# Where adding loads and other loads stand in the queues, and diagonal blocks masked by selects instead of products

## The chip, the cores and the metric

The kernel runs on one core of one Trainium2 chip. A core has five engines that run side by side, each through its own queue in order: TensorE (matrix products; PE in the rows below, its weight loads PEld), VectorE (DVE), ScalarE (ACT), GpSimd (POOL) and SyncE (SP). SyncE and GpSimd issue the transfers, which 16 DMA engines carry out. The metric is the device time of one execution in microseconds (us); lower is better. The kernel before takes 1485.59 us, the median of three runs (1484.99 to 1488.79).

## What is computed

A trunk of two layers on 512 positions of width 1024. Layer 0 mixes with an mLSTM, layer 1 with stick-breaking attention; each layer then cross-attends into 256 memory rows and applies a SwiGLU FFN. Each of these parts is normalised before and behind. Cut to the mixer that the change touches and to the frame:

```python
def reference(x, mem, ...):
    mem_n = rms_norm(mem, mem_norm_gain)
    for layer in range(2):
        hn = rms_norm(x, g[0])
        y = mlstm_mixer(hn, ...) if layer % 2 == 0 else stick_breaking_mixer(hn, ...)
        x = x + rms_norm(y, g[1])
        x = x + rms_norm(memory_cross_attention(rms_norm(x, g[2]), mem_n, ...), g[3])
        x = x + rms_norm(swiglu_ffn(rms_norm(x, g[4]), ...), g[5])

def mlstm_mixer(h, w_in, b_gate, head_gain, w_out):     # 4 heads, q and k 128 wide, v 256 wide
    q, k, v, o, gates = split(h @ w_in)                 # gates: 4 input, 4 forget, capped at 15
    ...                                                 # in each head, with b the running sum of log forget:
    # d[t, s] = exp(b_t - b_s + i_s - m_t) for s <= t, and 0 above the diagonal
    # num = ((q k^T) * d) v,  den = sum_s of (q k^T) * d,  out = num / max(|den|, exp(-m_t))
    return (rms_norm(out) * sigmoid(o)) @ w_out
```

The zero above the diagonal of `d` is the mask that the change makes in another way.

## The kernel before

Products are in fp32r, each factor split into a high part and a residual (`split`: a cast on ScalarE, a subtraction of 128x1024 on VectorE, "residual" below), so that a product is three matmuls.

**Units of seven products.** Large projections are cut into blocks of two by two and done with seven block products in place of eight, by `seven()`; there are 37 such units, numbered as they begin (mLSTM 0 to 4, cross-attention of layer 0 5 and 6, FFN of layer 0 7 to 20, then layer 1). A unit needs sums of weight blocks. It loads w00, w10 and w11 (128x1024 each, SyncE's queue) and forms the sums in place:

```python
self.gather(t1, src(1, 0))          # t1 = w00: DMA that adds w01 onto it, on GpSimd's queue
self.tt(t2, t1, w11, ALU.add)       # t2 = t1 + w11, VectorE
...
self.gather(t3, src(1, 0))          # t3 = w11: second adding DMA
...
if number in BY_DMA:
    self.gather(w10, t2)            # w10 += t2, by an adding DMA
else:
    self.tt(w10, w10, t2, ALU.add)  # or on VectorE
```

These DMAs are called adding loads here. The second one overwrites w11, so it can only be issued when t2 and the two halves of the old w11 have been formed. What it lands is split, and TensorE multiplies it.

**What sets the order.** The program isn't written in the order of its queues. `Plan` records every operation with its engine, a duration and the buffers that it reads and writes. `deadlines()` gives each a due time, counted back from the TensorE product that needs it; a load gets 2.5 us on top. `lay_out()` then fills each engine's queue by due time, as soon as inputs and a free buffer are there. The durations are the planner's own; on the chip an instruction waits only for what it reads, for its buffer and for its place in the queue.

**The mLSTM.** `MORDER` is the order in which its parts are written out; each letter advances one part by a step: `q`, `r` the projections of q and k for two heads each (units 0 and 2), `V` and `v` the values (unit 1 and a plain projection), `s` the scores of one head, `h` the heads' outputs for a block of 128 positions, `o` and `P` the two halves of the output gate (units 3 and 4). A unit has three steps. Then follow the loads and products of w_out.

**Masks and scores.** `masks()` makes constant tiles with `memset`, a select on GpSimd (it keeps or fills elements by their index) and a cast. One of them, `above`, holds a large number above the diagonal. `scores(hh)` needs for each pair of 128-blocks exp(-(row value) + column value). A product with `pick` spreads the row values of the head over the partitions, for blocks off the diagonal into one bank (384 columns), for those on it into a second (512 columns), onto which a product of the identity with `above` (512 columns) adds the large number, so that the exponential gives 0:

```python
self.mms([(mb[:, P:], self.pick[:, hh], rows[:, P:], True, True)])
self.mms([(md, self.pick[:, hh], rows, True, False), (md, self.ident_r, self.above, False, True)])
```

ScalarE takes ten exponentials of 128x128 per head from these banks; VectorE multiplies them with the products of q and k. There are eight banks (`ps`) in all.

Lines of the profile: L526 and L540 are TensorE's products and transposes, L470 VectorE's sums and products of two tiles, L482 its operations with a scalar in between, L448 and L455 ScalarE's functions and casts, L437 an adding load's issue, L432 another load's, L508 a select.

## Time and profile before

| | |
|---|---|
| median of three runs | 1485.59 us (1484.99 to 1488.79) |
| profiled execution, its device time | 1486.58 us |
| span of the profile | 1484.9 us |
| TensorE busy | 1469.4 us |
| VectorE busy | 1197.8 us |
| ScalarE busy | 865.8 us |
| GpSimd busy | 143.6 us |
| mean granted clock of TensorE | 0.997 of full speed |

The profile is one execution. Its span runs from the first instruction to the last; the device time lies 1.7 us above it. Busy time counts an engine's work, not its waits nor the issuing of DMAs from SyncE. The granted clock is given as a share: 1.00 is 2.4 GHz, 0.50 is 1.2 GHz. "Idle before" is the time that an engine stood still ahead of an instruction, with what ended it.

### The profile page before, as it was taken

What the parts mean: (1) busy time and instruction counts of PE and PEld (TensorE: products, weight loads), DVE (VectorE), ACT (ScalarE), POOL (GpSimd) and SP (SyncE); (2) the same over time, 40 slices, a digit from 0 to 9 for tenths busy, and PEclk for the clock granted to TensorE, in tenths of its full rate; (3) what the DMA queues carried; (4) which work ended last, traced back from release to release, by engine and by line L of the source; (5) the groups of instructions that cost most, each with busy time, mean ns of one, the idle gap of its engine ahead of it and who ended that gap; (6) DMA issues with size and microseconds to landing.
All of it is one profiled execution on the core that took longest, in us unless ns stands there. A gap on an engine that the chain in (4) does not pass through costs nothing.

```text
span 1484.9 us, 26101 instructions
## 1 busy us (share of the span) xinstructions
PE 1469.4 (99%) x10335; PEld 1370.6 (92%) x10335; DVE 1197.8 (81%) x1851; ACT 865.8 (58%) x1495; POOL 143.6 (10%) x179
## 2 busy tenths in 40 slices
PE   9999899999999999999999999999999999999998
PEld 7999889998999999998889889888988999999996
DVE  7988879887787877897838998878787968778985
ACT  7768656564654554544538997766546644444632
POOL 3100100100011111110100001001000111110100
PEclk9999999999999999999999999999999999999999
DMA  8445646532655575675343459255414563854741
GB/s 224 90 100 143 199 135 206 108 121 85 174 110 128 96 161 129 137 189 162 110 113 93 99 164 254 102 174 126 140 63 132 119 142 72 213 114 100 152 161 57
DMA packets 173228, 200.43 MB, mean 135 GB/s; under 512 B 8241, under 2 KB 142129, under 8 KB 173106
## 3 DMA queue, kind: packets, MB, share of 16 engines
q1 hardware_dynamic: 126192, 131.65, 28.8%
q0 software_dynamic: 46912, 67.12, 23.3%
q8 instruction: 81, 1.33, 0.4%
q14 instruction: 41, 0.34, 0.1%
q10 hardware_dynamic: 2, 0.00, 0.0%
HBM read 176.20 MB, written 10.49 MB: 126 GB/s over the span
## 4 chain that ended last, share of the span: by engine, by line
PE 94%; DMA 2%; DVE 2%; ACT 1%; issue 1%; DVEq 0%; POOL 0%; POOLq 0%; ACTq 0%
PE ps L526 92%; PE ps L540 2%; DMA big<-in_ffn_w_down_dram 1%; DVE big L470 1%; DMA big<-in_ml_w_in_dram 1%; ACT big L455 0%; DVE big L482 0%; ACT half L448 0%; DMA big<-in_norm_gains_dram 0%; DVE sm L475 0%; DVE half L470 0%; DVE sm L482 0%; ACT sm L448 0%; DVE big L456 0%; ACT half L455 0%
## 5 line engine op out<-in xcount | busy, mean ns | idle before, releaser
L526 PE MATMUL ps<-big,big 128*128 128x256 f32 (+2 forms) x9762 | 1407.4, 305 | 5.8 <-ACT big L455 2.8
L526 PEld LDWEIGHTS ps<-big,big 128*128 128x128 f32 (+1 forms) x9762 | 1298.0, 188 | 91.1 <-ACT big L455 3.3
L470 DVE TENSOR_TENSOR big<-big,big 128x1024 fp32r<-128x1024 f32 (+2 forms) x541 | 626.4, 1191 | 45.7 <-ACT big L455 25.1
L455 ACT CAST big<-big 128x1024 fp32r<-128x1024 f32 (+1 forms) x422 | 417.6, 1021 | 162.2 <-DMA big<-in_ffn_w_gate_up_dram 45.2
L470 DVE TENSOR_TENSOR big<-ps,big 128x512 fp32r<-128x512 f32 (+3 forms) x197 | 114.4, 605 | 44.2 <-ACT big L455 31.5
L455 ACT COPY half<-ps 128x512 f32<-128x512 f32 (+1 forms) x112 | 65.5, 585 | 124.1 <-PE ps L526 116.4
L455 ACT CAST big<-ps 128x512 fp32r<-128x512 f32 (+1 forms) x159 | 76.9, 513 | 99.6 <-PE ps L526 64.8
L448 ACT ACTIVATE half<-ps 128x512 f32<-128x512 f32 (+2 forms) x137 | 79.4, 581 | 90.2 <-PE ps L526 84.6
L448 ACT ACTIVATE half<-big 128x512 bf16<-128x512 f32 (+2 forms) x64 | 42.1, 659 | 73.0 <-DVE big L470 45.9
L437 POOL DMA_DIRECT2D big<-in_ffn_w_gate_up_dram x40 | 51.1, 1278 | 316.9 <-DVE big L470 217.4
L470 DVE TENSOR_TENSOR big<-half,big 128x512 fp32r<-128x512 f32 (+4 forms) x126 | 76.6, 625 | 5.9 <-ACT big L448 3.3
L482 DVE SCALAR_TENSOR_TENSOR half<-ps,half 128x512 f32<-128x512 f32 (+3 forms) x74 | 47.0, 645 | 36.4 <-PE ps L526 18.0
L455 ACT CAST big<-half 128x512 fp32r<-128x512 f32 (+3 forms) x82 | 43.9, 558 | 10.7 <-DVE half L470 6.3
L470 DVE TENSOR_TENSOR half<-ps,half 128x512 f32<-128x512 f32 (+1 forms) x54 | 36.4, 687 | 15.4 <-PE ps L526 11.9
L448 ACT ACTIVATE big<-ps 128x512 fp32r<-128x512 f32 (+2 forms) x66 | 39.6, 612 | 15.2 <-PE ps L526 11.8
L470 DVE TENSOR_TENSOR big<-ps,gain 128x512 f32<-128x512 f32 x32 | 22.0, 687 | 31.8 <-ACT half L448 30.0
L540 PE MATMUL ps<-const,big 128*128 128x128 f32 (+1 forms) x314 | 41.9, 270 | 0.8 <-DVE big L482 0.8
L540 PEld LDWEIGHTS ps<-const,big 128*128 128x128 f32 (+1 forms) x314 | 36.0, 140 | 6.0 <-DVE big L482 1.1
L475 DVE TENSOR_SCALAR sm<-sm,sm 128x1 f32<-128x1 f32 x101 | 24.2, 243 | 20.2 <-ACT half L448 11.4
L448 ACT ACTIVATE half<-half 128x512 f32<-128x512 f32 (+1 forms) x50 | 30.8, 630 | 10.3 <-DVE half L470 10.2
L482 DVE SCALAR_TENSOR_TENSOR big<-big,sm,gain 128x512 f32<-128x512 f32 (+1 forms) x45 | 34.9, 808 | 0.6
L482 DVE SCALAR_TENSOR_TENSOR big<-big,sm,big 128x512 f32<-128x512 f32 (+1 forms) x49 | 34.1, 737 | 0.8
(92 smaller groups left out, 588.2 us busy)
## 6 DMA issues: line engine op xcount, KB each, us to landing
big<-in_ffn_w_gate_up_dram SPq DMA_DIRECT2D x68, 512.0 KB, 5.0
big<-in_ffn_w_gate_up_dram POOLq DMA_DIRECT2D x40, 512.0 KB, 6.1
big<-in_ffn_w_down_dram SPq DMA_DIRECT2D x36, 512.0 KB, 5.9
big<-in_xa_w_kv_dram SPq DMA_DIRECT2D x32, 512.0 KB, 5.4
big<-in_sb_w_qkv_dram SPq DMA_DIRECT2D x24, 512.0 KB, 4.1
big<-big SPq DMA_DIRECT2D x80, 128.0 KB, 2.3
big<-in_ml_w_in_dram SPq DMA_DIRECT2D x18, 512.0 KB, 5.3
dr<-big POOLq DMA_DIRECT2D x16, 512.0 KB, 4.2
```

The costliest lines, as they stand in the source:

```text
L437: "POOL", 1040, lambda nc: nc.gpsimd.dma_start(ap(out), ap(in_), accum_op=ALU.add), [in_, out], [out], load=ns
L448: nc.scalar.activation(ap(out), ap(in_), func, scale=ap(scale), **kw)
L455: "ACT", 0.833 * n + (60 if psum else 95), lambda nc: nc.scalar.copy(ap(out), ap(in_)), [in_], [out],
L470: self._dve(out, [a, b], lambda nc: getattr(nc, q).tensor_tensor(out=ap(out), in0=ap(a), in1=ap(b), op=op), eng)
L475: nc.vector.tensor_scalar(out=ap(out), in0=ap(a), scalar1=ap(s1), scalar2=ap(s2), op0=op0, **kw)
L482: lambda nc: nc.vector.scalar_tensor_tensor(out=ap(out), in0=ap(a), scalar=ap(s), in1=ap(b), op0=op0, op1=op1),
L526: nc.tensor.matmul(ap(out), lhsT=ap(a), rhs=ap(b), start=start, stop=stop, **kw)
L540: nc.tensor.transpose(ap(out), ap(in_), ap(ident))
```

## The change

Three things are edited.

The planner's treatment of loads: an adding load's due time moves forward by `ahead` (6.5 us in the mLSTM, 4 in cross-attention, 7 in layer 0's FFN, 0.5 in layer 1's). Behind an adding load, a load of another kind that is due more than `NEAR` (11.75 us) ahead is laid out no sooner than 2 us before the adding load's planned end. Both are rules of the planner: the program gets no wait for them, only another order of its queues and other buffers.

Tables: in `MORDER` the second step of `o` stands ahead of the last head's scores, not behind it. `BY_DMA` gains units 0, 27 and 31. `LEAD` of the cross-attention's output loads goes from 3000 to 2000 (the entry 'cross', also edited, isn't read).

The mask: `above` is gone with its select and cast. `scores()` makes one product with `pick` over 512 columns into one bank, takes all exponentials from it, and a select on GpSimd sets each diagonal block's part above the diagonal to 0: four per head, 16 in all, 128x128 each. TensorE's instructions go from 10335 to 10327.

```diff
-MORDER = '+qqVqrsVVrrssosoohhPhhPP'
+MORDER = '+qqVqrsVVrrssoosohhPhhPP'
-BY_DMA = (3, 4, 18, 38, 39)
+BY_DMA = (0, 3, 4, 18, 27, 31, 38, 39)
+NEAR = 11750
+AHEAD = {'mlstm': 6500, 'cross': 4000, 0: 7000, 1: 500}
-LEAD = {'stick': 14000, 'ffn': 0, 'cross': 0, 'ml_out': 5500, 'sb_out': 2000, 'xa_out': 3000}
+LEAD = {'stick': 14000, 'ffn': 0, 'cross': 2000, 'ml_out': 5500, 'sb_out': 2000, 'xa_out': 2000}
...
     def deadlines(self):
-                o.rank = min(s.rank - (0 if s.eng == "PE" else s.ns) - 150 for s in o.succ) - o.ns - (2500 if o.load else 0)
+                o.rank = min(s.rank - (0 if s.eng == "PE" else s.ns) - 150 for s in o.succ) - o.ns - (2500 + o.ahead if o.load else 0)
...
     def lay_out(self):
             t = max(free[e], o.ready)
+            if o.load and e in ("SP", "POOL") and not o.adds and o.rank > headrank + NEAR:
+                t = max(t, quiet)
...
                 o.end = wire + 1500
+                if o.adds:
+                    quiet = o.end - 2000
...
     def gather(self, out, in_, ns=2800):
             "POOL", 1040, lambda nc: nc.gpsimd.dma_start(ap(out), ap(in_), accum_op=ALU.add), [in_, out], [out], load=ns
         )
+        self.plan.ops[-1].adds, self.plan.ops[-1].ahead = True, self.ahead
...
     def masks(self, behind):
-        self.above = self.half(NT, P, dt=R)
         self.strict = self.const(P, 2, P, dt=R)
-        for m, op, fill in ((self.above, ALU.is_ge, BIG), (self.strict, ALU.is_gt, -BIG)):
-            raw = self.half(*m.idx.shape)
-            self.memset(raw, 0.0, behind=[behind])
-            self.select(raw, op, fill, 0, [[0, m.idx.shape[0]], [1, P]], -1)
-            self.copy(m, raw)
+        raw = self.half(2, P)
+        self.memset(raw, 0.0, behind=[behind])
+        self.select(raw, ALU.is_gt, -BIG, 0, [[0, 2], [1, P]], -1)
+        self.copy(self.strict, raw)
...
         def scores(hh):
-            mb, md = self.bank(), self.bank()
-            self.mms([(mb[:, P:], self.pick[:, hh], rows[:, P:], True, True)])
-            self.mms([(md, self.pick[:, hh], rows, True, False), (md, self.ident_r, self.above, False, True)])
+            mb = self.bank()
+            self.mms([(mb, self.pick[:, hh], rows, True, True)])
...
                 for i in range(j, NT):
-                    src = (md if i == j else mb)[:, i * P : (i + 1) * P]
-                    self.act(dec[:, (i - j) * P : (i - j + 1) * P], src, AF.Exp, scale=-1.0, bias=col[(i, j)][:, hh : hh + 1])
+                    to, src = dec[:, (i - j) * P : (i - j + 1) * P], mb[:, i * P : (i + 1) * P]
+                    self.act(to, src, AF.Exp, scale=-1.0, bias=col[(i, j)][:, hh : hh + 1])
+                    if i == j:
+                        self.select(to, ALU.is_ge, 0.0, 0, [[1, P]], -1)
```

**GpSimd's queue in the mLSTM, units o and P.** In the kernel before, `big_1328` and `big_1281` are w11 and w10 of unit o, `big_1552`, `big_1666` and `big_1680` are w00, w10 and w11 of unit P, and `big_1950` is its t2.

```order
L437 DMA big_1328<-in_ml_w_in_dram 128x4x256
L437 DMA big_1281<-big_1455 128x1024
L437 DMA big_1552<-in_ml_w_in_dram 128x4x256
L437 DMA big_1666<-big_1950 128x1024
L437 DMA big_1680<-in_ml_w_in_dram 128x4x256
L432 DMA big_2060<-in_mem_dram 128x1024
L432 DMA big_2099<-in_mem_dram 128x1024
L432 DMA big_2116<-in_x_dram 128x1024
```

In the changed kernel w11 and w10 of unit o are `big_1305` and `big_1318`; of unit P w00, w10, w11 and t2 are `big_1607`, `big_1660`, `big_1676` and `big_1937`.

```order
L445 DMA big_1305<-in_ml_w_in_dram 128x4x256
L445 DMA big_1318<-big_1458 128x1024
L517 AFFINE_SELECT half_1582<-half_1582 128x128
L517 AFFINE_SELECT half_1613<-half_1613 128x128
L445 DMA big_1607<-in_ml_w_in_dram 128x4x256
L445 DMA big_1676<-in_ml_w_in_dram 128x4x256
L445 DMA big_1660<-big_1937 128x1024
L440 DMA big_2050<-in_mem_dram 128x1024
L440 DMA big_2095<-in_mem_dram 128x1024
```

Unit P's load onto w11 has moved ahead of its sum into w10, and selects now stand among the adding loads.

**VectorE's queue around unit P's t2.** In the kernel before, the rows onto `big_1617` are the last products of a heads' block, those onto `sm_1895` the denominators of the next block; `big_1950` is t2, and `big_1985` the residual of w11.

```order
L482 SCALAR_TENSOR_TENSOR big_1617<-ps_1800,sm_1857,gain_581 128x256
L470 TENSOR_TENSOR half_1878<-ps_1880,half_1878 128x512
L482 SCALAR_TENSOR_TENSOR sm_1895<-ps_1920,const_821 128x1
L470 TENSOR_TENSOR sm_1895<-ps_1920,sm_1895 128x1
L470 TENSOR_TENSOR big_1950<-big_1552,big_1680 128x1024
L482 SCALAR_TENSOR_TENSOR sm_1895<-ps_1937,const_821 128x1
L470 TENSOR_TENSOR sm_1895<-ps_1937,sm_1895 128x1
L482 SCALAR_TENSOR_TENSOR sm_1895<-ps_1956,const_821 128x1
L470 TENSOR_TENSOR sm_1895<-ps_1956,sm_1895 128x1
L492 RECIPROCAL sm_1980<-sm_1895 128x4
L470 TENSOR_TENSOR big_1985<-big_1680,big_1925 128x1024
```

In the changed kernel these are `big_1632`, `sm_1963`, `big_1937` (t2) and `big_1904` (the residual).

```order
L479 TENSOR_TENSOR big_1904<-big_1676,big_1876 128x1024
L491 SCALAR_TENSOR_TENSOR big_1632<-ps_1781,sm_1859,gain_574 128x256
L491 SCALAR_TENSOR_TENSOR big_1632<-ps_1793,sm_1859,gain_574 128x256
L479 TENSOR_TENSOR big_1937<-big_1607,big_1676 128x1024
L479 TENSOR_TENSOR half_1879<-ps_1863,half_1879 128x512
L491 SCALAR_TENSOR_TENSOR sm_1963<-ps_1900,const_814 128x1
L491 SCALAR_TENSOR_TENSOR sm_1963<-ps_1918,const_814 128x1
L491 SCALAR_TENSOR_TENSOR sm_1963<-ps_1933,const_814 128x1
L479 TENSOR_TENSOR sm_1963<-ps_1900,sm_1963 128x1
L491 SCALAR_TENSOR_TENSOR sm_1963<-ps_1947,const_814 128x1
```

The residual of w11 now stands ahead of t2, and both ahead of the next block's denominators.

**GpSimd's queue at the end of layer 0's FFN.** In the kernel before, rows from `in_ffn_w_down_dram` are the last units' adding loads, those from `dr` loads of the residual of x.

```order
L437 DMA big_7486<-in_ffn_w_down_dram 128x4x256
L437 DMA big_7492<-in_ffn_w_down_dram 128x4x256
L437 DMA big_7524<-in_ffn_w_down_dram 128x4x256
L432 DMA big_7845<-dr_4290 128x1024
L432 DMA big_7878<-dr_4409 128x1024
L432 DMA big_7911<-dr_4520 128x1024
L437 DMA big_7508<-in_ffn_w_down_dram 128x4x256
L432 DMA big_7939<-dr_4691 128x1024
```

In the changed kernel:

```order
L445 DMA big_7487<-in_ffn_w_down_dram 128x4x256
L445 DMA big_7493<-in_ffn_w_down_dram 128x4x256
L445 DMA big_7525<-in_ffn_w_down_dram 128x4x256
L445 DMA big_7509<-in_ffn_w_down_dram 128x4x256
L440 DMA big_7891<-dr_4288 128x1024
L440 DMA big_7930<-dr_4407 128x1024
L440 DMA big_7969<-dr_4518 128x1024
L440 DMA big_8002<-dr_4685 128x1024
```

The last adding load of w_down (`big_7508`, now `big_7509`) has moved ahead of three loads of the residual of x.

## Rows read from the trace of the kernel before

**Rows 1.** Page, part 1: busy us (share of span) and instructions of each engine.
```profile
PE 1469.4 (99%) x10335; PEld 1370.6 (92%) x10335; DVE 1197.8 (81%) x1851; ACT 865.8 (58%) x1495; POOL 143.6 (10%) x179
```

**Rows 2.** Stretches: us, busy us (count) per engine, PEclk, DMA share, GB/s.
```profile
120.00:140.00 20.00, 19.88 (x167) 19.67 (x166) 16.93 (x56) 17.02 (x37) 1.27 (x1) 1.00 0.62 150
160.00:180.00 20.00, 15.40 (x98) 14.22 (x97) 14.52 (x31) 15.79 (x28) 0.53 (x1) 0.83 0.62 232
680.00:700.00 20.00, 19.12 (x117) 16.94 (x118) 17.35 (x22) 9.61 (x13) 0.00 (x0) 1.00 0.40 134
1460.00:1480.00 20.00, 17.86 (x95) 15.11 (x93) 12.07 (x33) 5.41 (x18) 0.00 (x0) 1.00 0.14 53
```

**Rows 3.** Timeline of TensorE: start, us, what, [idle before <-releaser].
```profile
164.43 0.58 PE L526 MATMUL ps<-big,big 128*128 128x256 f32 x1 [2.81 <-ACT big L455]
165.69 5.23 PE L526 MATMUL ps<-big,big 128*128 128x256 f32 x23 [0.68 <-DVE big L470]
171.59 5.99 PE L526 MATMUL ps<-big,big 128*128 128x256 f32 x48 [0.67 <-ACT half L455]
```

**Rows 4.** Stretches of 6 and 8 us at unit P.
```profile
158.00:164.00 6.00, 3.17 (x27) 2.73 (x25) 3.44 (x10) 1.10 (x3) 0.53 (x1) 0.99 1.10 343
164.00:172.00 8.00, 6.22 (x27) 5.68 (x28) 5.73 (x7) 7.71 (x15) 0.00 (x0) 0.58 0.86 349
```

**Rows 5.** Chain of waits up to 166 us: start, us, what.
```profile
150.17 13.14 DMA big<-in_ml_w_in_dram
...
163.33 1.05 ACT big L455
...
164.41 1.24 DVE big L470
```

**Rows 6.** Timeline of VectorE, same columns as rows 3.
```profile
143.24 0.87 DVE L482 SCALAR_TENSOR_TENSOR big<-ps,sm,gain 128x256 f32<-128x256 f32 x2
...
146.48 1.23 DVE L470 TENSOR_TENSOR big<-big,big 128x1024 f32<-128x1024 f32 x1
```

**Rows 7.** Timeline of GpSimd's issues, same columns.
```profile
114.12 1.26 POOL L437 DMA_DIRECT2D big<-in_ml_w_in_dram  x1 [8.81 <-DVE half L482]
...
148.36 0.87 POOL L437 DMA_DIRECT2D big<-big  x1 [13.89 <-ACT half L448]
```

**Rows 8.** DMA issues, 148 to 171: count, KB each, median us to landing.
```profile
big<-in_x_dram POOLq DMA_DIRECT2D x4, 512.0 KB, 13.2
big<-in_mem_dram POOLq DMA_DIRECT2D x2, 512.0 KB, 13.7
...
big<-in_ml_w_in_dram POOLq DMA_DIRECT2D x1, 512.0 KB, 13.1
```

**Rows 9.** DMA issues, 112 to 126 (unit o).
```profile
big<-in_ml_w_in_dram POOLq DMA_DIRECT2D x1, 512.0 KB, 5.9
big<-big POOLq DMA_DIRECT2D x1, 512.0 KB, 8.1
```

**Rows 10.** DMA issues, 666 to 682 (end of FFN of layer 0).
```profile
big<-in_ffn_w_down_dram POOLq DMA_DIRECT2D x1, 512.0 KB, 10.9
big<-dr POOLq DMA_DIRECT2D x1, 512.0 KB, 11.9
```

**Rows 11.** Chain of waits: a projection of 48 products, 512 wide.
```profile
358.66 11.13 PE ps L526 x48
```

**Rows 12.** Chain of waits ahead of unit P's first product.
```profile
137.14 0.40 DVE big L482
...
137.59 8.09 PE ps L526 x66
```

**Rows 13.** Groups of GpSimd: line, engine, what xcount | busy us, mean ns | idle.
```profile
L508 POOL TENSOR_SCALAR_AFFINE_SELECT half<-half 128x128 f32<-128x128 f32 x2 | 0.6, 286 | 0.0
```

**Rows 14.** Stretch in which the masks are made.
```profile
22.00:28.00 6.00, 6.00 (x40) 5.36 (x39) 6.00 (x8) 3.78 (x8) 5.86 (x10) 1.00 0.73 121
```

**Rows 15.** Timeline of ScalarE: the last head's exponentials.
```profile
116.56 2.89 ACT L448 ACTIVATE half<-ps,const 128x128 f32<-128x128 f32 x10 [0.45 <-PE ps L526]
```

More of the change, by code (lines that the diff above doesn't have):

```diff
@@ L140 @@
 class Op:
-    __slots__ = ("eng", "ns", "fn", "deps", "succ", "rank", "bufs", "news", "table", "wait", "start", "end", "load", "seq", "ready", "base", "alts", "lead")
+    __slots__ = ("eng", "ns", "fn", "deps", "succ", "rank", "bufs", "news", "table", "wait", "start", "end", "load", "seq", "ready", "base", "alts", "lead", "ahead", "adds")
 class Plan:
@@ L167, in op @@
         o.rank = o.base = self.pe + self.bias
-        o.lead = self.lead
+        o.lead, o.adds, o.ahead = self.lead, False, 0
         o.deps, o.succ, o.bufs, o.news = set(), [], [], []
@@ L213, in lay_out @@
         free = dict.fromkeys(self.LATENCY, 0.0)
-        table, wire = "ln_exp", 0.0
+        table, wire, quiet = "ln_exp", 0.0, 0.0
         cand = {e: [] for e in free}
@@ L395, in __init__ @@
         self.kept = None
-        self.sevens = 0
+        self.sevens = self.ahead = 0
     def big(self, *shape, dt=F32):
@@ L1686, in after_mixer @@
             nxt["f"](n, t, ps)
+        k.ahead = AHEAD["mlstm"]
         if layer % 2 == 0:
@@ L1700, in after_cross @@
             nxt2["f"](n, t, ps)
+        k.ahead = AHEAD["cross"]
         k.cross(XORDER[layer], h, nxt["m"], kt, filler, xa_w_q[layer], xa_w_kv[layer], xa_w_o[layer], after_cross)
@@ L1714, in after_ffn @@
             return k.boundary(xs, g(layer, 5), g(layer + 1, 0), nxt3["h"], ys=ys, spill=nxt3["x"])
+        k.ahead = AHEAD[layer]
         k.ffn(UNITS[layer], h, ffn_w_gate_up[layer], ffn_w_down[layer], after_ffn, layer == depth - 1)
```

## Prediction

> **What bounds the kernel now.** I read the busy times first: TensorE 1469.4 of 1484.9 us, VectorE 1197.8 [rows 1]. TensorE sets the time, so the question for every edit is whether it takes work from TensorE or closes one of its gaps. The gaps add up to 1484.9 - 1469.4 = 15.5 us. The stretches of 20 us say where they are [rows 2]: 4.6 us between 160 and 180, 0.9 between 680 and 700, 0.1 between 120 and 140, 2.1 between 1460 and 1480, and the last 4.9 us, in which TensorE is done. The change doesn't touch the tail, so two places count.
>
> The first is mLSTM unit P, the output gate's second half. TensorE stops at 161.6, starts one matmul at 164.43, goes on at 165.69 and once more at 171.59 [rows 3]. Its clock is 0.99 up to 164 and 0.58 on average in the eight us behind [rows 4], so for much of them it ran at 1.2 GHz; just before, it had stood still. There 23 matmuls took 5.23 us, 227 ns each; 48 of the same kind from 171.59 on took 5.99 us, 125 ns each [rows 3]. The low clock cost 23 x (227 - 125) = 2.4 us, and the place 4.6 + 2.4 = 7.0 us.
>
> The chain of waits says who is late: the second adding load of unit P (the DMA that adds w01 onto w11) is issued at 150.17 and takes 13.14 us; then come a cast of 1.05 and a subtraction of 1.24 [rows 5]. Why 150.17? VectorE must form the sum t2 from w11 before the load overwrites it, and did so at 146.48 [rows 6], behind rows of the heads; then came the residual of w11, and on GpSimd's queue the sum into w10 at 148.36 [rows 7]. Why 13.14? Two loads of mem and four of x were under way in those 23 us beside others, and those of x were as slow (13.2 us) [rows 8]. The same kind of load in unit o, issued at 114.12 [rows 7], landed in 5.9 us [rows 9].
>
> The second place is the end of layer 0's FFN: the 0.9 us of idle time lie behind an adding load of w_down that took 10.9 us, with a load of the residual beside it [rows 10].
>
> **The change part by part.**
>
> *Unit P.* The orders show it: the residual of w11 and t2 now stand ahead of block 2's denominators on VectorE, and the load onto w11 ahead of the sum into w10 on GpSimd. In the trace the four head products that stay ahead of t2 ended at 144.1 [rows 6]. With the residual in front (1.2 us, the length of a 1024-wide row [rows 6]) t2 would run from about 145.3 to 146.5 and the load be issued at about 147, 3 us sooner. Its landing I bound by 5.9 us (unit o) and 13.14 us (as now) [rows 5, 9]: 153 to 160. With 1.05 + 1.24 us and hand-overs the data are there between 155.5 and 162.7. TensorE arrives at 161.6, or at some 161 with the work below gone. So the stop of 4.6 us becomes 0 to 1.8 us. I take 0.3, near unit o's row: there too the sum into w10 was the neighbour, and the loads of mem and x stay behind both on GpSimd's queue. The stop of 0.9 us at 680 left the clock at 1.00 [rows 2], so I take the 2.4 us as regained. Gain: 7.0 - 0.3 = 6.7 us, bounds 5.2 and 7.0.
>
> That loads are "held back" is a rule of the planner; no wait for it is put into the program. It acts only through the order of each queue and the buffers that the plan picks, so I give it no gain of its own.
>
> *FFN of layer 0.* The last adding load of w_down stood behind three loads of the residual and now stands ahead of all four. Gain 0 to 0.9 us; I take 0.8.
>
> *Masks.* Per head the products of 384 and 512 columns with `pick` and of 512 columns with the identity become one of 512. Four of 512 and four of 384 go. At the pace of a 512-wide projection, 48 in 11.13 us or 232 ns [rows 11], that is 4 x 0.232 + 4 x 0.174 = 1.6 us of TensorE's work. It is of use only if nothing else sets the pace behind. At 137.59 the first product of unit P started right behind a VectorE row of the heads that frees a bank [rows 12], and TensorE had 0.1 us of idle time there [rows 2]: that row was only just late. TensorE now arrives 1.6 us sooner, the rows of VectorE and ScalarE that lead to it hardly do. I let 1.0 of the 1.6 us be given back there (bounds 0 and 1.6). Net gain: 0.6 us.
>
> *Selects.* Sixteen selects of 128x128 come to GpSimd, each between ScalarE's exponential and VectorE's product. One takes 0.29 us [rows 13], 4.6 us in all on an engine that is a tenth busy [rows 1]. The heads read the scores some ten us or more behind, and each head holds a bank less than now. I cost them at nothing; that distance is the cover. Without it each is 0.29 us and a hand-over of some 0.1: 16 x 0.4 = 6.4 us at most. The adding loads that queue behind them are the rival below.
> One of the two selects of that size ran beside the mask work between 22 and 28, where VectorE was busy 6.00 of 6 us [rows 14]; the mean of both is 0.29 us all the same. The Trainium skill, "SBUF — State Buffer", section "SBUF: two separate sides", speaks against this edit: GpSimd and VectorE share a pair of ports that one instruction locks for its whole length, a VectorE instruction with two SBUF inputs among them, and the other engine waits. By it each select could wait for a 1024-wide row, some 20 us on GpSimd in all, or hold VectorE up for 4.6 us; the rows of this size show no such wait, and off TensorE's path the sum would be the same.
>
> *Three more sums by DMA.* Units 0, 27 and 31 leave their sum into w10 to a DMA; VectorE saves 1.23 us each [rows 6], where it isn't the bound. The cost is an issue on GpSimd and a DMA beside the unit's second adding load, which in unit o landed in 5.9 us with such a neighbour [rows 9]. I take nothing, and up to 1 us of loss each at 27 and 31, where the sum is queued ahead of that load. All other loads that move: nothing, and up to 2 us of loss together, for the range.
>
> **Sum.** Against the profiled execution: 1484.9 - 6.7 - 0.8 - 0.6 = 1476.8 us of span. That execution took 1.7 us more than its span and 1.0 us more than the median of the three runs. Against the median: 1485.6 - 8.1 = 1477.5 us.
>
> **The rivals.**
> *The load stays slow.* The same bytes go through the same DMA engines, which had hardly a free moment from 158 on [rows 4]. If the load still takes 13 us and t2 comes no sooner, only its place in the queues (1 to 2 us) is won; the stop is then some 3 us and the clock falls again: 1485.6 - 2 - 0.8 - 0.6 = 1482. For it: the landing times of x [rows 8]; against it: those loads now queue behind. Chance 0.14.
> *The gap moves.* VectorE was busy 14.5 us between 160 and 180 [rows 2]; with 7 us less, that work must fit into 13 us, or TensorE stops for the splits of w_out instead, with the low clock behind. If the place gives back 6 us: 1483.5. Against it: part of that work belongs to the projection behind and can be done there. Chance 0.08.
> *Slower.* The adding loads of units r, o and P now queue behind selects, and a select waits for its exponential. In unit o the load was issued at 114.12 [rows 7], while the last head's ten exponentials ran only from 116.56 to 119.45 [rows 15]. A load held until then is up to 5.3 us late; if TensorE waits as long and then runs at the low clock (2.4 us), that is 7.7 us. At one load it eats the gain (1485); at two the kernel is slower: 1477.5 + 15.4 = 1493. It decides from 12.5 us of such losses. Against it: in the new order the last head's product with `pick` stands right behind the third's, so its exponentials can run sooner. Chance 0.05.
> *The change doesn't do what it says:* waits that no plan sees swallow the moves, and only the masks' 0.6 us stay, 1485. Chance 0.05.
>
> **How the numbers follow.** The forecast has 0.68: 1477.5, its own range 1474.8 (less if nothing is given back at the bank) to 1480.5 (a stop of 1.8 us and a loss at other loads). 0.3% is 4.5 us, about what a measurement of this kernel can tell from no change, so faster means under 1481.1 and slower over 1490.1. Faster: 0.68 and half of the slow load's 0.14, 0.75. Slower: 0.05. Same: 0.20. The range leaves out the slower case, half of the last one and some 0.05 below: 1474.5 to 1485.
>
> **What would show it.** Right: between 155 and 175 TensorE idles under 1 us and its clock stays at 1.00; the adding load of unit P is issued some 3 us sooner against TensorE's work and lands in under 10 us; no idle time near 680; about 1 us of idle time ahead of unit P's first product; 16 selects of about 0.3 us. Wrong: a clock under 1.00 anywhere but the start and the tail, or an adding load of unit o or P issued right behind a select that waited.

## The result

The changed kernel takes 1477.84 us, the median of six runs (1476.74 to 1482.79); the kernel before took 1485.36 in its six (1484.98 to 1488.79). The ratio is 0.9950, with a 95% interval of 0.9934 to 0.9966: 7.4 us less (5.1 to 9.8). The forecast was 1477.5, within 1474.5 to 1485.0.

The profile after, first its part 1 (columns as in rows 1), its span being 1476.3 us:

```profile
PE 1465.3 (99%) x10327; PEld 1367.7 (93%) x10327; DVE 1197.2 (81%) x1854; ACT 864.5 (59%) x1490; POOL 155.6 (11%) x196
```

TensorE's busy time fell by 4.1 us, its idle time from 15.5 to 11.0. Three stretches of 20 us, beside rows 2:

```profile
120.00:140.00 20.00, 18.98 (x159) 18.76 (x158) 17.58 (x53) 18.84 (x41) 3.37 (x3) 1.00 0.57 126
160.00:180.00 20.00, 20.00 (x141) 18.43 (x140) 19.72 (x53) 15.30 (x31) 0.53 (x1) 1.00 0.70 263
680.00:700.00 20.00, 20.00 (x103) 16.77 (x102) 14.95 (x31) 8.21 (x22) 0.54 (x1) 1.00 0.15 52
```

Between 160 and 180 TensorE no longer stops and its clock stays at 1.00, where 4.6 us of idle time and 0.83 stood. Between 120 and 140 it now stands still for 1.0 us. The timeline of TensorE shows both, beside rows 3:

```profile
138.45 24.53 PE L535 MATMUL ps<-big,big 128*128 128x256 f32 x204 [1.02 <-DVE big L491]
162.82 1.47 PE L549 MATMUL ps<-const,big 128*128 128x128 f32 x12
164.05 5.91 PE L535 MATMUL ps<-big,big 128*128 128x256 f32 x48
169.80 1.47 PE L549 MATMUL ps<-const,big 128*128 128x128 f32 x12
171.03 3.73 PE L535 MATMUL ps<-big,big 128*128 128x512 f32 x15
```

138.45 is unit P's first product, 171.03 the first of w_out; in the kernel before these stood at 137.59 [rows 12] and 178.21. GpSimd's issues there, beside rows 7, and unit P's second adding load among the DMA issues from 145 to 171, beside rows 8:

```profile
147.53 1.28 POOL L445 DMA_DIRECT2D big<-in_ml_w_in_dram  x1 [12.99 <-DVE big L479]
148.28 1.43 POOL L445 DMA_DIRECT2D big<-big  x1
151.53 0.98 POOL L440 DMA_DIRECT2D big<-in_mem_dram  x1 [1.81 <-PE ps L535]
```

```profile
big<-in_ml_w_in_dram POOLq DMA_DIRECT2D x1, 512.0 KB, 6.1
```

The load is issued ahead of the sum into w10, 9.1 us behind unit P's first product in place of 12.6 [rows 5, 12], and lands in 6.1 us in place of 13.14.

**Where the time is counted.** The first 37 to 40 us of the program, in which its first loads arrive, differ by up to 3 us from profile to profile whatever the kernel, and what comes behind the mLSTM (from the first product of w_out to the last product) lay between 1298.3 and 1300.2 us in all fourteen profiles, with a kernel made from the one before at either end (e5 and e1). I therefore also compare one stretch: from the product behind the short wait that every profile shows near 38 (37.09 in the kernel before, 38.60 in the changed one) to the first product of w_out. It took 178.21 - 37.09 = 141.1 us before and 171.03 - 38.60 = 132.4 after: 8.7 us less. Profiles of three kernels with the same order of queues there (the changed one, e6 and e12) gave 132.43, 132.47 and 132.43, so it tells tenths apart.

### The profile page after: what moved, and what is told of

The parts are those of the page before. It is cut to its first block, busy times and chain, and to the rows that moved or that the text cites. A ratio compares the mean times of both kernels' runs of the same rounds, so it can differ in the third digit from the quotient of the medians.

```text
span 1476.3 us, 26092 instructions
## 1 busy us (share of the span) xinstructions
PE 1465.3 (99%) x10327; PEld 1367.7 (93%) x10327; DVE 1197.2 (81%) x1854; ACT 864.5 (59%) x1490; POOL 155.6 (11%) x196
## 3 DMA queue, kind: packets, MB, share of 16 engines
q8 instruction: 81, 1.33, 0.4%
## 4 chain that ended last, share of the span: by engine, by line
PE 97%; DVE 1%; ACT 1%; issue 0%; DVEq 0%; POOL 0%; ACTq 0%; POOLq 0%
PE ps L535 95%; PE ps L549 2%; DVE big L479 0%; DVE big L491 0%; ACT big L464 0%; ACT half L457 0%; DVE sm L484 0%; ACT L358 0%; ACT sm L457 0%; DVE sm L491 0%; DVE big L465 0%; DVEq L1753 0%; ACTq L440 0%; ACT const L464 0%; POOL half L512 0%
## 5 line engine op out<-in xcount | busy, mean ns | idle before, releaser
L479 DVE TENSOR_TENSOR big<-big,big 128x1024 fp32r<-128x1024 f32 (+3 forms) x538 | 622.7, 1191 | 46.4 <-ACT big L464 22.4
L464 ACT CAST big<-big 128x1024 fp32r<-128x1024 f32 (+2 forms) x421 | 417.4, 1022 | 152.1 <-DMA big<-in_ffn_w_gate_up_dram 51.4
L479 DVE TENSOR_TENSOR big<-ps,big 128x512 fp32r<-128x512 f32 (+3 forms) x197 | 114.3, 605 | 43.4 <-ACT big L464 31.0
L491 DVE SCALAR_TENSOR_TENSOR half<-ps,half 128x512 f32<-128x512 f32 (+1 forms) x74 | 46.9, 644 | 24.3 <-ACT half L464 15.0
L464 ACT CAST big<-half 128x512 fp32r<-128x512 f32 (+1 forms) x82 | 43.8, 559 | 17.7 <-DVE half L479 10.5
L457 ACT ACTIVATE half<-half 128x512 f32<-128x512 f32 (+1 forms) x50 | 30.8, 630 | 12.7 <-DVE half L479 12.6
L445 POOL DMA_DIRECT2D big<-in_ffn_w_down_dram x16 | 20.5, 1280 | 145.7 <-DVE big L479 108.1
```

What stands on the lines that cost most here:

```text
L445: "POOL", 1040, lambda nc: nc.gpsimd.dma_start(ap(out), ap(in_), accum_op=ALU.add), [in_, out], [out], load=ns
L457: nc.scalar.activation(ap(out), ap(in_), func, scale=ap(scale), **kw)
L464: "ACT", 0.833 * n + (60 if psum else 95), lambda nc: nc.scalar.copy(ap(out), ap(in_)), [in_], [out],
L479: self._dve(out, [a, b], lambda nc: getattr(nc, q).tensor_tensor(out=ap(out), in0=ap(a), in1=ap(b), op=op), eng)
L491: lambda nc: nc.vector.scalar_tensor_tensor(out=ap(out), in0=ap(a), scalar=ap(s), in1=ap(b), op0=op0, op1=op1),
```

## The experiments

The table has all of them: the ratio to the kernel before, the stretch just described, when unit P's second adding load was issued and landed (from the stretch's start), and TensorE's stops behind unit P's first product. The times of the last columns are worked out from each kernel's timelines.

| kernel | ratio | stretch | issued | landed | stops |
|---|---|---|---|---|---|
| before | 1 | 141.1 | 113.1 | 126.2 | 0.44, 2.81, 0.68, 0.67 |
| changed | 0.9950 | 132.4 | 108.9 | 115.0 | none |
| e1 before, P's load due sooner | 0.9987 | 138.3 | 111.6 | 121.3 | 0.64, 2.61 |
| e2 changed, P's load due as before | 0.9968 | 134.9 | 111.1 | 120.4 | 2.10 |
| e3 before, two issues exchanged | 1.0027 | 144.6 | 113.1 | 122.7 | 8.04, 0.68 |
| e4 changed, exchanged back | 0.9950 | 133.0 | 109.5 | 117.8 | none |
| e5 before, mem and x wait | 0.9997 | 140.8 | 113.1 | 125.9 | 0.71, 2.19, 0.68, 0.68 |
| e6 changed, nothing held back | 0.9949 | 132.5 | 108.9 | 115.1 | none |
| e7 changed, old steps | 0.9952 | 132.9 | 109.1 | 118.6 | none |
| e8 changed, old masks | 0.9976 | 135.2 | 110.9 | 118.2 | none |
| e9 before, w_out waits | 0.9972 | 135.9 | 113.0 | 120.0 | 0.44, 1.03, 0.68 |
| e10 before, new masks | 0.9990 | 138.6 | 111.3 | 124.3 | 4.07, 0.68 |
| e11 before, new masks, P's load due sooner | 0.9945 | 131.3 | 107.8 | 113.9 | none |
| e12 changed, FFN's loads due as before | 0.9946 | 132.4 | 108.9 | 114.8 | none |

My theory was the prediction's: the load onto w11 is late since it is issued late, behind the sum. The rival was that the loads beside it make it slow.

### e1: unit P's due time alone

The kernel before, with `ahead` in the due time of this one load:

```diff
...
+        self.ahead = 6500 if number == 4 else 0
         self.gather(t3, src(1, 0))
+        self.ahead = 0
```

> The kernel before, with one thing of the change: the due time of unit P's second adding load moves 6.5 us forward. Its queues then have the residual of w11 ahead of t2 and the load ahead of the sum into w10; masks, other adding loads and all other rules are those of before. Theory 'order' (the load was late because it was issued late and behind the sum): the load is issued some 2 to 3 us sooner and lands in about 6 us, TensorE doesn't stop near 160, and the time falls by 7 to 8 us to 1477.5 to 1478.5. Rival 'held back' (the load was slow because of loads of w_out, mem and x beside it, and only holding those back helps): the load still takes 11 us or more, 1 to 3 us of gain, 1482.5 to 1484.5. Rival 'whole change' (only the change's parts together do it): no difference, 1485.4.

Measured: 0.9987 (0.9978 to 0.9995), 1.9 us less. On GpSimd the load now stands ahead of the sum, and on VectorE the residual ahead of t2, but TensorE still stops, and its clock falls behind the stop. Timeline of TensorE, then its stretches (columns as in rows 2), then the load among the DMA issues:

```profile
164.07 4.34 PE L527 MATMUL ps<-big,big 128*128 128x256 f32 x24 [2.61 <-ACT half L456]
```

```profile
160.00:164.00 4.00, 1.46 (x13) 1.22 (x11) 3.04 (x10) 3.94 (x9) 0.00 (x0) 1.00 1.01 376
164.00:168.00 4.00, 3.93 (x24) 3.94 (x24) 3.90 (x9) 3.49 (x7) 0.53 (x1) 0.69 1.03 408
```

```profile
big<-in_ml_w_in_dram POOLq DMA_DIRECT2D x1, 512.0 KB, 9.7
```

The load came only 1.4 us sooner, not 3. The timeline of VectorE shows why:

```profile
143.24 0.16 DVE L483 SCALAR_TENSOR_TENSOR sm<-ps,const 128x1 f32<-128x1 f32 x1 [0.41 <-ACT half L449]
...
144.32 0.16 DVE L483 SCALAR_TENSOR_TENSOR sm<-ps,const 128x1 f32<-128x1 f32 x1 [0.85 <-ACT half L449]
...
146.68 2.35 DVE L471 TENSOR_TENSOR big<-big,big 128x1024 fp32r<-128x1024 f32 x2
```

VectorE waits twice for ScalarE in rows of the heads, and the residual with t2 (the last row) follows only at 146.68. The two rows that wait are denominators of the next block: three of its four stand ahead of the residual here, none in the changed kernel. So the due time alone doesn't give VectorE's queue the order of the changed kernel.

What ends the stop of 2.61 us is not the load's own split but a copy of ScalarE out of a bank. It stands in ScalarE's queue behind the cast of what the load lands, for which ScalarE stood still (its timeline):

```profile
159.34 1.05 ACT L456 CAST big<-big 128x1024 fp32r<-128x1024 f32 x1 [4.59 <-DMA big<-in_ml_w_in_dram]
```

Neither theory as I had put it holds: the moved due time brings a quarter of the gain.

### e2: the same due time put back in the changed kernel

```diff
+        keep = self.ahead
+        self.ahead = 0 if number == 4 else keep
         self.gather(t3, src(1, 0))
+        self.ahead = keep
```

> The changed kernel, with the due time of unit P's second adding load put back, and nothing else. Theory 'order': the load stands behind the sum again and the stop near 160 comes back with its low clock, so the time is 7 to 8 us above the changed kernel, 1485 to 1486. Rival 'held back': the loads beside it are still held back, the stop stays away, 1478 to 1480.

Measured: 0.9968 (0.9957 to 0.9980), 2.7 us above the changed kernel. The stop comes back in part, and without the low clock (timeline of TensorE, and a stretch behind the stop):

```profile
161.81 3.00 PE L535 MATMUL ps<-big,big 128*128 128x256 f32 x23 [2.10 <-DVE big L479]
```

```profile
162.00:166.00 4.00, 4.00 (x36) 4.00 (x36) 3.90 (x11) 4.00 (x8) 0.53 (x1) 1.00 1.04 409
```

The intervals of the two ratios overlap; the stretch, 134.9 against 132.4, tells them apart. So with this one due time as before, some 4.8 of the 7.4 us stay. Something else in the change carries much of the gain.

### e3 and e4: only two issues exchanged

In the order laid out, unit P's load onto w11 and its sum into w10 change places on GpSimd, once in the kernel before and once in the changed one:

```diff
         self.gather(t3, src(1, 0))
+        third = self.plan.ops[-1]
...
             self.gather(w10, t2)
+            if number == 4:
+                self.plan.pair = third, self.plan.ops[-1]
...
+        a, b = sorted(self.pair, key=order.index)
+        order.remove(a)
+        order.insert(order.index(b) + 1, a)
         self.order, self.ns = order, max(o.end for o in order)
```

> The kernel before, with only two issues on GpSimd's queue exchanged: unit P's load onto w11 is issued ahead of the sum into w10, on VectorE and everywhere else nothing moves. The load then waits for the residual of w11, which ended at 149.55, so it is issued 0.5 us sooner, not 3. If the place in the queue counts (the sum's transfers ahead of the load's): it lands in about 6 us, at 156, the stop goes, 1477.5 to 1478.5. If the time of issue counts: still about 13 us, a gain of 0.5 us, 1484.5 to 1485.5. By 'held back' the same as that, 1485.

> The changed kernel, with only the same two issues exchanged back: the sum into w10 first, then unit P's load onto w11, so the load is issued about 0.8 us later, at 148.3, still 1.9 us sooner than in the kernel before. If the place in the queue counts most: it takes about 13 us, is there after cast and subtraction at 163.7, the stop is 2 us or more with a low clock behind, 1481 to 1484. If the time of issue counts most: 8 to 9 us as the second of the pair, there at 159.5, no stop, 1477.5 to 1478.5.

Measured: 1.0027 (1.0017 to 1.0038), 4.0 us slower, and 0.9950 (0.9937 to 0.9962), as the changed kernel. In e3 the load lands in 9.6 us in place of 13.1, so the place in the queue is worth 3.5 us to it; but the load couldn't be issued sooner, since it waits for the residual, and the sum behind it now lands in 12.1 us. In ScalarE's queue the cast of that sum stands ahead of rows of the heads, and so those wait too, and TensorE's transposes behind them (timelines of ScalarE and of TensorE):

```profile
165.36 1.04 ACT L458 CAST big<-big 128x1024 fp32r<-128x1024 f32 x1 [7.51 <-DMA big<-big]
```

```profile
170.43 1.94 PE L543 MATMUL ps<-const,big 128*128 128x128 f32 x8 [8.04 <-DVE big L485]
```

In e4, with the sum and the load issued 2.3 and 3.6 us sooner than before, it doesn't matter which is first: the load lands in 8.3 us as the second of the pair, 117.8 us behind the stretch's start, and TensorE doesn't stop. In e3 the pair is done no sooner than in the kernel before (126.0 against 126.2 us behind the start), and there the order costs 4.0 us. So the order doesn't matter where both land early. The moved queue position, on which the prediction rested as much as on the time, is no gain by itself.

### e5 and e9: what makes the load slow

In e5 a select on GpSimd that reads what the load lands stands ahead of the issues of mem and x, so that these wait. In e9 ScalarE writes a corner of each tile of the second half of w_out from what has landed, so that these four loads on SyncE's queue wait. VectorE's order up to t2 and the load's issue are those of before in both.

```diff
         self.gather(t3, src(1, 0))
+        if number == 4:
+            third = self.plan.ops[-1]
+            tiny = self.half(128)
+            self.plan.op("POOL", 250, lambda nc: nc.gpsimd.affine_select(
+                out=ap(tiny), in_=ap(t3[:, 0, 0:128]), compare_op=ALU.is_ge, fill=0.0, base=0, pattern=[[1, P]], channel_multiplier=-1), [t3], [tiny])
+            self.plan.pair = third, self.plan.ops[-1]
...
```

```diff
         raw = self.plan.buf("big", (P,) + shape)
+        if self.behind is not None:
+            a, b = raw[:, 0, 0:128], self.behind[:, 0, 0:128]
+            self.plan.op("ACT", 200, lambda nc: nc.scalar.copy(ap(a), ap(b)), [b], [a])
         self.dma("SP", raw, src)
...
+                self.behind = self.third if n and lead == LEAD['ml_out'] else None
...
+        if number == 4:
+            self.third = w11
```

> The kernel before, with one instruction more: a select of 128x128 on GpSimd, behind unit P's second adding load, that reads what it lands. The issues of the two loads of mem and the four of x, which stand behind it in GpSimd's queue, so wait until it has landed; VectorE's order, t2 and the load's own issue (12.6 us behind unit P's first product) stay. Theory 'crowded' (the load takes 13 us since mem and x, issued right behind it, share the DMA engines): it lands in 6 to 9 us, from unit P's first product to the first of w_out it takes 33 to 36 us where it took 40.6, and the time is 1478 to 1481. Rival 'sooner' (only an earlier t2 helps): it lands in 11 us or more, 1483 to 1485.5. Third: the late loads of mem hold ScalarE up, a new stop of 2 us or more, 1484 to 1488.

> The kernel before, with the four loads of the second half of w_out held until unit P's second adding load has landed: ScalarE writes a corner of each of their tiles from what has landed, which costs four instructions of about 0.3 us. Loads of mem and x stay as they are, and so do t2 and the load's issue, 12.6 us behind unit P's first product. Holding mem and x back left the landing time at 12.8 us, and SyncE's queue carried most of the bytes in the meantime. Theory 'w_out crowds it': the load lands in 7 to 10 us instead of 13, the stop near 160 falls from 4.6 us to 0 to 1.5, and from the stretch's start at 37 to the first product of w_out it takes 135 to 138 us where it took 141.1; the total is 1479 to 1483, more if the second half of w_out is then late. Rival 'GpSimd's queue works the two adding DMAs off one behind the other at a fixed pace': 12 us or more, no difference, 1485 to 1487.

Measured: e5 0.9997 (0.9988 to 1.0006), no difference; e9 0.9972 (0.9961 to 0.9983), 4.2 us less. The load among the DMA issues from 148 to 171, of e5 and then of e9:

```profile
big<-in_ml_w_in_dram POOLq DMA_DIRECT2D x1, 512.0 KB, 12.8
```

```profile
big<-in_ml_w_in_dram POOLq DMA_DIRECT2D x1, 512.0 KB, 6.9
```

Both kernels issue it 113.1 us behind the stretch's start, to a tenth. With mem and x out of the way it is as slow as ever; with w_out out of the way it takes 6.9 us, though mem and x are issued right behind it. What the DMA engines moved from 154 to 158 says the same (queue, packets, MB, share of 16 engines; q0 is GpSimd's queue, q1 SyncE's), in e5 and then in e9:

```profile
q1 hardware_dynamic: 528, 1.02, 68.5%
q0 software_dynamic: 186, 0.18, 28.4%
```

```profile
q0 software_dynamic: 592, 1.33, 112.6%
```

Loads of w_out on SyncE's queue took two thirds of the engines' time and left GpSimd's queue 0.18 MB, where it moved 1.33 MB alone, part of that plain loads of mem behind the adding load. What is issued on GpSimd's queue behind a transfer landed behind it in every one of these traces. That two queues share each engine, which turns from one to the other packet by packet, is what the Trainium skill says ("DMA: Bandwidth & Descriptors", section "Queues, rings and completion order"). The traces agree: from 158 to 160 of e5 the two queues moved as many packets, but the adding ones are half as large.

```profile
q0 software_dynamic: 180, 0.18, 57.2%
q1 hardware_dynamic: 178, 0.36, 55.4%
```

In e9 the stop shrinks to 1.03 us and two shorter waits, and no low clock follows: 23 products behind it take 2.97 us, 129 ns each.

```profile
162.52 2.97 PE L527 MATMUL ps<-big,big 128*128 128x256 f32 x23 [1.03 <-DVE big L471]
```

### e6 and e7: no hold, old steps

```diff
-NEAR = 11750
+NEAR = 10**9
```

```diff
-MORDER = '+qqVqrsVVrrssoosohhPhhPP'
+MORDER = '+qqVqrsVVrrssosoohhPhhPP'
```

> The changed kernel without the rule that holds other loads back behind an adding load; due times, masks and tables stay. In unit P's queues the order stays, only the buffers differ that the loads of mem and x take, and so the time at which they can start. The prediction gave this rule nothing: 1477.5 to 1478.5. By 'crowded', if those loads now start within 1 us of unit P's pair: it lands 2 to 4 us later, and as the changed kernel has some 3 us in hand there, 1478 to 1480.5.

> The changed kernel with the old order of steps: the gate's second step behind the last head's scores again. On GpSimd the sum into w10 then stands ahead of unit P's load again, with t2 as in the changed kernel. The prediction gave this table nothing by itself. Theory 'sooner': VectorE comes to t2 and the residual 1 us or more later, the stop near 160 comes back in part, 1479.5 to 1482.5. Theory that due times and hold alone carry the gain: 1477.5 to 1478.8.

Measured: 0.9949 (0.9937 to 0.9962) and 0.9952 (0.9939 to 0.9964), both as the changed kernel, the stretch 132.5 and 132.9. Neither the rule that holds loads back nor the moved step is worth anything that can be measured.

### e8 and e10: the masks

e8 is the changed kernel with `masks()` and `scores()` of before, e10 the kernel before with those of the change:

```diff
...
-            mb = self.bank()
-            self.mms([(mb, self.pick[:, hh], rows, True, True)])
+            mb, md = self.bank(), self.bank()
+            self.mms([(mb[:, P:], self.pick[:, hh], rows[:, P:], True, True)])
+            self.mms([(md, self.pick[:, hh], rows, True, False), (md, self.ident_r, self.above, False, True)])
...
```

> The changed kernel with the old masks: the products onto the diagonal blocks are back, the 16 selects gone; due times, hold and tables stay. By the prediction's sum the masks are worth 0.6 net (1.6 us of TensorE's work less what is given back at the bank ahead of unit P): 1478.2 to 1479. Rival: the masks carry part of unit P's gain, since TensorE and VectorE stand otherwise to each other there, and the stop comes back: 1480 to 1483. Without the selects nothing else should get faster; if it is below 1477.5, the selects cost more than they save.

> The kernel before with the new masks alone: one product with pick for each head, 16 selects, no other edit. By the prediction's sum: 0.6 us less than before (1.6 of TensorE's work, 1.0 given back ahead of unit P), 1484.5 to 1485.3. Undoing the masks in the changed kernel cost 2.8 us of that stretch, so the rival is 'masks and due times need each other': alone they bring 0 to 1 here since the stop near 160 takes up what TensorE gains. Third: 2.8 us here too, 1482.5 to 1483.5.

Measured: e8 0.9976 (0.9966 to 0.9986), 3.9 us above the changed kernel; e10 0.9990 (0.9981 to 0.9999), 1.5 us below the one before. In the stretch, undoing them costs 2.8 us and doing them alone gains 2.5. 1.6 of that is TensorE's work: its 512-wide products in the stretch went from 44 to 40 at 0.23 us, those of 384 from 16 to 12 at 0.18. Another 0.39 us in e8 is a stop at 88.85 that the changed kernel doesn't have; the remainder I have not traced. The wait ahead of unit P's first product, which I had laid to the masks, is there without them, in e8, and gone with them alone, in e10 (timelines of TensorE):

```profile
139.78 10.41 PE L535 MATMUL ps<-big,big 128*128 128x256 f32 x85 [1.04 <-DVE big L491]
```

```profile
119.83 30.45 PE L526 MATMUL ps<-big,big 128*128 128x256 f32 x252
```

In e10 TensorE runs without a wait through the place, and stops later, for the load, which again took 13 us:

```profile
162.71 0.58 PE L526 MATMUL ps<-big,big 128*128 128x256 f32 x1 [4.07 <-ACT big L455]
```

### e11: two parts alone

The kernel before with e10's masks and e1's due time, and nothing else of the change.

> The kernel before with two parts of the change: the new masks, and the due time of unit P's second adding load moved 6.5 us forward. Everything else is that of before: steps, tables, other due times, no hold. The load stands ahead of the sum, t2 and the residual ahead of the next denominators, as in the changed kernel. If these two parts carry the gain: no stop near 160, 1477.5 to 1479.5. If the due times of the mLSTM's other units are needed (they bring VectorE to t2 sooner): a stop of 1 to 3 us stays, 1480 to 1483.

Measured: 0.9945 (0.9932 to 0.9958), 8.2 us less; the changed kernel has 0.9950. These two parts carry the whole gain, though each alone brings 1.5 and 1.9 us. Stretches beside rows 2:

```profile
120.00:140.00 20.00, 19.93 (x168) 19.73 (x167) 17.72 (x56) 15.78 (x39) 1.27 (x1) 1.00 0.52 121
160.00:180.00 20.00, 19.90 (x133) 17.77 (x132) 18.60 (x51) 15.28 (x31) 0.53 (x1) 1.00 0.69 253
```

No stop and no low clock, and not the 1.0 us ahead of unit P either: the stretch is 131.3, 1.1 us shorter than the changed kernel's. In the whole time the two can't be told apart. VectorE forms the residual and t2 ahead of all four denominators of the next block, and so without the waits for ScalarE that e1 shows:

```profile
143.36 2.35 DVE L471 TENSOR_TENSOR big<-big,big 128x1024 fp32r<-128x1024 f32 x2
```

That is 104.9 us behind the stretch's start, where e1 has 108.7. Why the planner lays three of those denominators ahead with the old masks, and none with the new, I have not isolated; the second bank that each head then holds is my guess.

### e12: the FFN's due times

```diff
-AHEAD = {'mlstm': 6500, 'cross': 4000, 0: 7000, 1: 500}
+AHEAD = {'mlstm': 6500, 'cross': 4000, 0: 0, 1: 500}
```

> The changed kernel with the due times of layer 0's FFN put back: the last adding load of w_down stands behind three loads of the residual again. The prediction's term: a stop of 0.8 to 0.9 us near 675 comes back, 1478.5 to 1479.2. Rival: two of the kernels with the old order there showed no stop at that place, so it comes and goes with the landing times, and nothing changes, 1477.5 to 1478.4.

Measured: 0.9946 (0.9933 to 0.9959), as the changed kernel. A stop of 0.53 us is there again, near 672:

```profile
672.16 18.21 PE L535 MATMUL ps<-big,big 128*128 128x256 f32 x112 [0.53 <-DVE big L479]
```

Of the kernels with the order of before at this place, four showed a stop there (0.88, 0.82 in e1, 0.34 in e9 and this 0.53), and four none (e3, e5, e10 and e11). Of the six others with the moved load (the changed one, e2, e4, e6, e7 and e8) none showed one. So with the old order the stop comes and goes, the new order may well take it away, and 0.3 to 0.9 us aren't seen in the whole time.

## Why the prediction was right, and where it wasn't

**The total and the place** were right: the stop at unit P and its clock are gone, 7 us of the time were there, and the rest is small. But of the steps behind it some were wrong, and errors of opposite sign met: that the sum of 8.1 us came so near to the 7.4 measured is in part luck. The lower end of the forecast's own range, 1474.8, doesn't follow from its terms; with no stop, 0.9 us at the FFN and nothing given back they reach 1476.1.

*Unit P, 6.7 forecast.* From unit P's first product to the first of w_out it took 40.62 us and takes 32.58: 8.0 less. 4.60 of it are the stops, as I had read them; the other 3.4 I had at 2.4. The 23 products at 227 ns were right: 5.23 us, where as many take 2.73 after. Mis-sized is what each stop costs beside its idle time: the single product between two of them took 0.58 us [rows 3] in place of 0.12, and the 24 transposes, cut apart by two stops, 2.88 in place of 2.46.

*What makes the load slow.* I named mem and x, whose landing times were as long [rows 8]. e5 refutes that, e9 shows w_out. The long times of mem and x were an effect of the same cause: they stood in the same queue. I had seen that DMA engines were busy [rows 4] and didn't ask which queue filled them.

*Why it now lands in time.* "The load 3 us sooner" came true (3.5 us against unit P's first product). But I ascribed it to the moved due time alone and worked it out from rows of the kernel before with its masks. e1 shows that this step gives 1.4 us there, e10 that the masks give 1.8 us, and e11 that together they give 5.3 (113.1 to 107.8). The rival "the load stays slow", at 0.14, is near to what the due time alone does: 9.7 us, a stop, a low clock. The rows of SyncE's issues suggest why so much hangs on a few us, in the kernel before and in the changed one:

```profile
149.05 0.37 SPq L432 DMA_DIRECT2D big<-in_ml_w_out_dram  x1
```

```profile
151.62 0.37 SPq L440 DMA_DIRECT2D big<-in_ml_w_out_dram  x1
```

In the kernel before a load of w_out is issued 1.1 us ahead of unit P's load, in the changed one the last of those ahead has landed at 148.2, the next is issued 4.1 us behind unit P's load, and the packets that moved between 149 and 152 were all of GpSimd's queue. In e1 and e10 a load of w_out is 1.1 and 0.8 us ahead again (9.7 and 13.0 us to landing), in e6 and e11 the next is 2.7 us behind (6.1 us). The first of them is issued 110.5 to 114.3 us behind the stretch's start in all but e9, and the two edits of e11 together bring unit P's load out in front of it. That they make it slow e9 shows; that this order is all that the two edits need was not tested by itself.

*Masks, 0.6 forecast.* The work of 1.6 us was right to a tenth. That 1.0 was given back at the bank was right in sum for the wrong reason: the wait of 1.02 us comes with the other edits (e7, with 1.43, e8 and e12 have it, e10 and e11 don't). And a gain of TensorE in front was worth more than its own length, since the heads' rows and t2 move up with it (t2 by 1.7 us in e10).

*FFN of layer 0, 0.8 forecast.* Not found in the whole time: e12. The term rested on one profile of a stop that four of the eight profiles of the same order don't show; with the new order it is absent in all six.

*Held loads, sums by DMA, steps: nothing forecast.* Right for the hold (e6) and the steps (e7). The sums by DMA were not tried by themselves; e11 leaves them out with the rest and is no slower, and what lies behind the mLSTM took as long in all profiles.

*Selects.* "0.29 us each" and "the rows of this size show no such wait" were wrong as a forecast. The group of GpSimd's selects after, and three rows of its timeline and VectorE's:

```profile
L517 POOL TENSOR_SCALAR_AFFINE_SELECT half<-half 128x128 f32<-128x128 f32 x18 | 11.0, 617 | 36.0 <-ACT half L457 26.6 <-issue 6.0 <-DVE big L479 3.3
```

```profile
103.91 1.13 POOL L517 TENSOR_SCALAR_AFFINE_SELECT half<-half 128x128 f32<-128x128 f32 x1 [4.70 <-ACT half L457]
```

```profile
103.68 1.22 DVE L479 TENSOR_TENSOR big<-big,big 128x1024 fp32r<-128x1024 f32 x1
```

```profile
109.18 0.29 POOL L517 TENSOR_SCALAR_AFFINE_SELECT half<-half 128x128 f32<-128x128 f32 x1 [2.10 <-ACT half L457]
```

The 18 of this size, the 16 new ones and two others, take 0.62 us in the mean. The one at 103.91 began while VectorE ran a row with two inputs in SBUF, up to 104.90, and ended 0.14 us behind it; the one at 109.18, beside a row that reads a bank, took 0.29. That is the rule of the Trainium skill ("SBUF — State Buffer", section "SBUF: two separate sides") which I had weighed and set aside by two selects of the kernel before: of a VectorE instruction with two SBUF inputs and an instruction of GpSimd that reads SBUF, the one that starts first locks the other out for its whole length. The sum didn't move by it: no stop of TensorE in the changed kernel was ended by a row that a select had just released.

*The list of signs.* Idle time under 1 us between 155 and 175, the clock at 1.00, the load 3 us sooner and landed in under 10, nothing near 680, and 1 us ahead of unit P's first product came true. The length of the selects did not. Of the signs of being wrong one came up as well: unit o's first adding load, at 105.43, was issued right behind two selects, the first of which had waited 4.70 us for ScalarE. It came no later behind the stretch's start than before (66.83 us, before 66.95), and TensorE didn't stop before the 1.02 us ahead of unit P, so this sign meant nothing here.

## What to carry to other kernels

When a transfer is slow, ask by queue what the DMA engines moved meanwhile, and test it by holding back one queue's loads at a time: the neighbour in the same queue, with the same long landing time, was innocent here. An edit that comes a little sooner on a path that just misses its date can be worth little alone and much together with another; price such edits as a sum of lead against the date, not one by one, and then drop the rest (two of the edits carried this change). A stop of TensorE can cost more than its idle time, above all where a low clock follows it.

## What was not expected of the hardware

Adding loads move few bytes for the engines' time: between 150 and 152 of the kernel before the DMA share was 1.05 at 191 GB/s (0.92 of it and 0.29 of 0.38 MB an adding transfer, the rest plain), between 164 and 166, with plain loads, 1.02 at 418 GB/s.

```profile
150.00:152.00 2.00, 2.00 (x19) 2.00 (x19) 2.00 (x7) 1.96 (x5) 1.83 (x2) 1.00 1.05 191
164.00:166.00 2.00, 0.90 (x2) 0.60 (x3) 1.59 (x2) 2.00 (x3) 0.00 (x0) 0.50 1.02 418
```

And where plain loads of SyncE's queue ran beside them, GpSimd's queue got 0.18 MB of 1.2 in 4 us (e5). After a stop of 2.10 us the clock stayed at 1.00 (e2), after one of 2.61 us the stretch behind it shows 0.69 (e1), and after 2.81, 0.68 and 0.67 us 0.58 [rows 4].
